# Silu rows at their written place, other PSUM banks and weight slots around attention, and whole quarters in the last opening of a two-layer diffusion backbone

## The chip, the cores and the metric

The kernel runs on one core of one Trainium2 chip, in one launch. The metric is device time of that core in microseconds. The kernel before was run three times: 2442.37, 2443.3 and 2446.17, a median of 2443.3.

## What is computed

Two layers work on 512 latent tokens and a prefix of 256 context tokens, 1024 channels each. Every layer is a half-step SwiGLU, a token mixer (layer 0 a short gated convolution, layer 1 attention with 8 query and 2 key heads of 128) and a second half-step SwiGLU of width 2816. Each of the six sub-layers is an RMSNorm, a shift and scale from a conditioning vector, the sub-layer, and a gated residual. After attention only the latent tokens are left.

```
def norm_modulate(x, g, shift, scale):
    return rms_norm(x, g) * (1 + scale) + shift

def swiglu(h, w_in, w_out):
    gate, up = jnp.split(h @ w_in, 2, axis=-1)
    return (jax.nn.silu(gate) * up) @ w_out
...
        m_lat = (silu_c @ ada_w[i] + ada_b[i]).reshape(b, N_SUBLAYERS, N_MOD, 1, d)
...
        h = norm_modulate(x_lat, norm_g[i, 0], m_lat[:, 0, 0], m_lat[:, 0, 1])
        x_lat = x_lat + MACARON_WEIGHT * m_lat[:, 0, 2] * swiglu(h, ffn_w_in[i, 0], ffn_w_out[i, 0])
...
            y_lat, y_ctx = attention_mixer(h, hc, attn_w_qkv[j], attn_q_g[j], attn_k_g[j], attn_w_o[j],
                                           cos, sin, not last)
...
    return rms_norm(x_lat, final_g)
```

## The kernel before

**Numbers.** Everything is float32. A product is made of three TensorE matmuls (`mm3`, L814 to L816): each operand is split into a high part in TensorE's own 32-bit format, which ScalarE writes by a copy (L186), and a low part, the remainder, which VectorE writes by a subtraction (L187). high × high, low × high and high × low are added up in PSUM. So each weight tile and each activation tile costs ScalarE and VectorE an instruction before TensorE can use it.

**Stages.** They run one after the other under the keys f00 (first SwiGLU, with the start of the kernel, the boot), c01 (convolution), f02, f10, attention, and f12, the last SwiGLU. Large products are taken by Strassen's seven products M1 to M7 over halves of the channels and halves of the tokens; their operands are sums such as T1 to T4 of the four quarters B11, B21, B12 and B22 of the modulated input (first digit: half of the channels, 4 chunks of 128; second digit: half of the tokens). A half of the tokens is 384 up to f10 and 256 in f12. The first few columns of each stage (c0, c1, in the boot c2) are multiplied directly, by quarters, while the sums are still being made.

**Opening.** The norm, the modulation and the splits of a stage are its opening. Per quarter: `normed` (L732, VectorE, x times the root), `modulated` (L745, ScalarE, one instruction for each chunk), `parted` (L769 ScalarE high, L771 VectorE low). Each of these works on pairs of chunks, `PAIRS`: 2 × 384 = 768 elements for each partition, or 2 × 256 = 512 in f12. The sums of quarters (L774) and their splits go by pairs, too. `OPENING` and `behind` in `out_close` list at which step of the products each call stands. The squares (`sq_add`, `ssq`) and the root (`th`, `tl`, `y`, `r`, L589 to L617) come before, for each half of the tokens when its residuals (L882, L952) are done.

**Weights.** SyncE's queue fetches raw weights in 512 KB pieces into 5 `raw` buffers. ScalarE and VectorE split them into 8 buffers `w` (granules of 128 x 512), or into slots of a large buffer (`T0` to `T13`) that other tiles have left. `stream` is their order; an entry with an event isn't split before the event has been traced. `oheld` are six of the output weights of attention's second half of heads, with the event "heads", which is traced at the end of attention. `HELD_AFTER_HEADS` names their slots. `add_out` lists the weights of the down projections, whose first part covers two chunks of the width and whose others cover four (`FFN_PARTS`); an entry for a part of two is 128 x 256.

**Conditioning.** Products of later shifts, scales and gates run on VectorE in the background (L510, `ada_step`), paced behind the products. They need `silu_row`, a row of Silu(c) for each half of its length: GpSimd's queue brings it, ScalarE makes the Silu in place (L495). ScalarE needs its Silu table for it; the root needs the table of Ln and Exp, so it reloads when it turns from one to the other (1283 ns each). The gate of a SwiGLU needs the Silu table as well.

**Order.** TensorE and SyncE's queue run in the written order. VectorE runs in the written order along its chain. ScalarE's instructions are placed by a scheduler, except inside the regions that `in_order` opens (the boot's opening, `out_close` with the opening behind it, the end). So a Silu of a background row can be placed earlier than it is written.

**PSUM.** It has eight banks, given to pools by name: `psum(C=2, O=1)` opens two tiles C of two banks and one bank O, and later pools lie over banks of closed ones in the order in which they are opened. The rotary stage of attention holds Q, two B, four A and S. Attention proper (`scores` L1447, `turn` L1470, `values`) then takes 32 blocks, 4 for each of 8 heads: scores into C, softmax by VectorE and ScalarE into `pr`, six transposes through T into `p`, and every second block the product with the values into O. From the second half of the heads on, T is given up and opened anew beside two banks AB, in which the output projection of the first four heads runs, one output for each block (`filler`). `out_close` then takes the second four heads' part, in two halves of the tokens, with f12's opening behind it.

Of the kernel before, what the change touches and what calls it, by code (L numbers as in the profile page):

```python
# [18 lines left out]
P = 128  # L19
D = 1024  # L20
KC = D // P
# [48 lines left out]
LAST_T_SLOTS = {**T_SLOTS, "T1": (12, 13), "T3": (6, 7)}  # L70
LAST_F_SLOTS = {**F_SLOTS, (0, 0): 6, (1, 0): 7}
HELD_AFTER_LAST_T = ((12, 13), (10, 11), (8, 9))
HELD_AFTER_HEADS = ((4, 5), (8, 9))
# [53 lines left out]
def backbone(ctx: ExitStack, tc: tile.TileContext, a: dict, out: bass.AP):  # L127
# [266 lines left out]
    def w_list():  # L394
# [25 lines left out]
        add_out(a["attn_w_o"], 4, 4, HELD_AFTER_HEADS, "oheld", ("heads", "heads"))  # L420
# [70 lines left out]
    def silu_load(kh):  # L491

        row = silu_row[kh] = apool.tile([P, 2, 512], F32, name=f"silu_row{kh}", tag="acc")
        nc.gpsimd.dma_start(row, a["crow"][kh].unsqueeze(0).to_broadcast((P, 2, 512)))
        act.activation(row, row, AF.Silu)  # L495
# [212 lines left out]
    PAIRS = (slice(0, 2), slice(2, 4))  # L708
# [10 lines left out]
    def opening(i, s):  # L719
# [6 lines left out]
        def normed(half, tok, p):  # L726

# [3 lines left out]
            m = 4 * half + PAIRS[p].start  # L731
            dve.tensor_tensor(out=full[half, tok][:, PAIRS[p]], in0=xs(slice(m, m + 2), off, n), in1=rs[geo.tokens[tok]].unsqueeze(1).to_broadcast((P, 2, n)), op=ALU.mult)  # L732

        def modulated(half, tok, p, mode=None):

            off, n = geo.tokens[tok]
            for k in range(PAIRS[p].start, PAIRS[p].stop):
# [24 lines left out]
        def parted(half, tok, p, which="both", more=0):  # L762
            name = f"B{half + 1}{tok + 1}"
            if p == 0 and which != "lo":
                t_tiles(name, more)
            hi, lo = T[name][0][:, PAIRS[p], : geo.half], T[name][1][:, PAIRS[p], : geo.half]
            src = full[half, tok][:, PAIRS[p]]
# [5 lines left out]
        def minus(o, x, y, p):  # L773
            dve.tensor_tensor(out=o[:, PAIRS[p]], in0=x[:, PAIRS[p]], in1=y[:, PAIRS[p]], op=ALU.subtract)  # L774

        def sums(which, p):
            if which == "T1":
# [12 lines left out]
        def sum_parted(which, p):  # L790
            if p == 0:
                t_tiles(which)
            t_split(which, full[which] if which in full else full[0, 0], PAIRS[p])
# [67 lines left out]

    def out_steps(groups, passes, gh, gl, npart, after, alloc, width):
# [23 lines left out]
        for m0 in range(0, KC, width):  # L886
            ms = range(m0, min(m0 + width, KC))
            units = [w_get() for _ in ms]
# [10 lines left out]
            else:  # L899
# [4 lines left out]
                w_done()  # L904
# [384 lines left out]
    def attention(gp, i, s):  # L1289
# [140 lines left out]
        with tc.tile_pool(name="core", bufs=2) as cp, psum(C=2, O=1), ExitStack() as more:  # L1430
            more.enter_context(psum(T=3))
# [3 lines left out]
            def scores(h, blk):  # L1435
                g = h // 4
                if blk == 0:
# [3 lines left out]
                    st[h] = qh, ql  # L1441
                qh, ql = st[h]
# [19 lines left out]
            def turn(h, blk, pr):  # L1462
# [4 lines left out]
                for c0 in (0, 3):  # L1467
                    pt = ptile("T", (P, 4, P))[:, :3, :]
# [25 lines left out]
            for n, (h, blk) in enumerate(blocks):  # L1494
# [19 lines left out]
            traced.add("heads")  # L1514
# [207 lines left out]
    with tc.tile_pool(name="g2", bufs=1) as gp, tc.tile_pool(name="qp2", bufs=1) as qp, psum(C=3, A=3, B=1, S=1):  # L1722
# [77 lines left out]
```

## Time and profile before

| What | us |
|---|---|
| Median of three runs | 2443.3 |
| The profiled execution | 2442.06 |
| Its span | 2439.9 |
| TensorE's loading of weights busy, beside its matmuls | 2264.6 |
| ScalarE, L186, all splits of weights (868) | 524.9 |
| VectorE, L187, all splits of weights (868) | 577.6 |
| VectorE, L510, conditioning (416) | 313.8 |
| TensorE's longest wait: the first transfer, ada, at the start | 4.3 |

The profiled execution is one run; its span reaches from the first to the last instruction and is 2.16 us shorter than its time. The matmul ends of TensorE are modelled by the profiler, so a busy TensorE may still run slower than it could where its clock is throttled; the granted clock beside a window shows that. In lists of waits a line says which engine, on which line, waited for the result of which other engine and line, with the total, how often, and the longest. Numbers of lines are those of the kernel before.

### The profile page before, as it was taken

Reading aid. Unit: us, or ns where it says so; the run is one execution under the profiler, and the core shown is the slowest. Engines: PE = TensorE matmul, PEld = TensorE weight load, DVE = VectorE, ACT = ScalarE, POOL = GpSimd, SP = SyncE. Lnnn points to the kernel's source line nnn. Section 1 sums busy time; section 2 is a strip of 40 time slices with the busy share of each in tenths; the row PEclk is TensorE's granted clock in tenths of the full one; section 3 lists DMA queues with packets and bytes.
Section 4 is the critical chain, followed back from the end, with each engine's and each line's share of the span. In section 5 each row is a group of like instructions: output and inputs, shape, how many; then the busy total and the mean of one; then the engine's idle time right before and its main releaser. Section 6 shows DMA issues by size and latency. Waiting matters only on the chain.

```text
span 2439.9 us, 37626 instructions
## 1 busy us (share of the span) xinstructions
PE 2396.1 (98%) x14303; PEld 2264.6 (93%) x14303; DVE 2031.1 (83%) x4011; ACT 1166.9 (48%) x2205; POOL 134.6 (6%) x256
## 2 busy tenths in 40 slices
PE   8999999999999999999999999999999999999998
PEld 5899999999999999999999999999997889899997
DVE  5889989978988888888877988788768887887776
ACT  5544344356435643443435534334346776555545
POOL 0001101100000001001000011101100000000000
PEclk9999999999999999999999999999999999999999
DMA  8234433330334023323431134434331101132232
GB/s 312 87 113 125 140 129 122 126 130 26 100 106 133 30 71 115 123 94 114 130 105 60 66 117 132 153 118 136 128 113 61 44 1 48 57 115 102 99 102 78
DMA packets 93061, 253.70 MB, mean 104 GB/s; under 512 B 10320, under 2 KB 18640, under 8 KB 92880
## 3 DMA queue, kind: packets, MB, share of 16 engines
q1 hardware_dynamic: 71984, 183.65, 22.2%
q0 software_dynamic: 20352, 67.12, 8.9%
q8 instruction: 112, 1.84, 0.3%
q14 instruction: 69, 0.57, 0.1%
q10 hardware_dynamic: 544, 0.52, 0.1%
HBM read 249.16 MB, written 2.10 MB: 103 GB/s over the span
## 4 chain that ended last, share of the span: by engine, by line
PE 80%; issue 8%; DVE 6%; ACT 4%; DMA 2%; POOL 0%; SPq 0%; DVEq 0%; ACTq 0%; POOLq 0%
PE ps_A L815 14%; PE ps_A L814 14%; PE ps_A L816 14%; PE ps_C L814 9%; PE ps_C L815 9%; PE ps_C L816 9%; PE ps_B L816 3%; PE ps_B L814 2%; PE ps_B L815 2%; DVE w L187 1%; PE ps_T L1470 1%; DMA raw<-in_ffn_w_in 1%; DMA silu_row<-in_crow 0%; DMA ada<-in_ada_w 0%; ACT f L745 0%
## 5 line engine op out<-in xcount | busy, mean ns | idle before, releaser
L186 ACT ACTIVATE w<-raw 128x512 fp32r<-128x512 f32 (+1 forms) x868 | 524.9, 619 | 735.8 <-PE ps_A L816 294.8
L187 DVE TENSOR_TENSOR w<-raw,w 128x512 fp32r<-128x512 f32 (+1 forms) x868 | 577.6, 679 | 129.6 <-ACT w L186 117.4
L489 POOL DMA_DIRECT2D aw<-in_ada_t x240 | 129.0, 538 | 1389.4 <-DVE mods L510 985.6
L814 PE MATMUL ps_C<-gh,w 128*128 128x512 f32 (+1 forms) x544 | 194.0, 357 | 3.3 <-ACT w L186 2.8
L815 PE MATMUL ps_C<-gl,w 128*128 128x512 f32 (+1 forms) x544 | 193.8, 356 | 0.0
L816 PE MATMUL ps_C<-gh,w 128*128 128x512 f32 (+1 forms) x544 | 193.5, 356 | 0.0
L354 DVE TENSOR_TENSOR raw<-raw,raw 128x512 f32<-128x512 f32 x264 | 181.3, 689 | 11.2 <-DMA raw<-in_ffn_w_in 7.2
L814 PE MATMUL ps_A<-gh,w 128*128 128x256 f32 (+1 forms) x544 | 180.6, 332 | 1.2 <-DVE x L882 1.2
L816 PE MATMUL ps_A<-gh,w 128*128 128x256 f32 (+1 forms) x544 | 180.7, 332 | 0.0
L815 PE MATMUL ps_A<-gl,w 128*128 128x256 f32 (+1 forms) x544 | 180.6, 332 | 0.0
L510 DVE CUSTOM_DVE_ANT_0 ps_S<-aw,silu_row,packed 128x512 f32<-128x512 f32 x208 | 156.9, 754 | 2.2 <-DMA aw<-in_ada_t 0.9
L510 DVE CUSTOM_DVE_ANT_0 ps_S<-aw,silu_row,mods 128x512 f32<-128x512 f32 x208 | 156.9, 754 | 1.0
L882 DVE SCALAR_TENSOR_TENSOR x<-ps_C,gat,x 128x512 f32<-128x512 f32 (+1 forms) x156 | 102.8, 659 | 41.3 <-PE ps_C L816 41.0
L814 PE MATMUL ps_A<-tB11h,w 128*128 128x384 f32 (+1 forms) x400 | 130.7, 327 | 0.2 <-ACT tB11h L754 0.2
L815 PE MATMUL ps_A<-tB11l,w 128*128 128x384 f32 (+1 forms) x400 | 130.4, 326 | 0.2 <-DVE tB11l L755 0.2
L816 PE MATMUL ps_A<-tB11h,w 128*128 128x384 f32 (+1 forms) x400 | 130.4, 326 | 0.0
L815 PE MATMUL ps_C<-tB22l,w 128*128 128x384 f32 (+2 forms) x384 | 124.6, 325 | 0.0
L816 PE MATMUL ps_C<-tB22h,w 128*128 128x384 f32 (+2 forms) x384 | 124.2, 324 | 0.0
L814 PE MATMUL ps_C<-tB22h,w 128*128 128x384 f32 (+2 forms) x384 | 124.0, 323 | 0.0
L814 PEld LDWEIGHTS ps_C<-gh,w 128*128 128x128 f32 x544 | 103.2, 190 | 18.1 <-ACT w L186 4.4
L814 PE MATMUL ps_A<-tT4h,w 128*128 128x384 f32 (+1 forms) x352 | 114.2, 325 | 2.9 <-DVE c L1091 2.9
L882 DVE SCALAR_TENSOR_TENSOR x<-ps_A,gat,x 128x512 f32<-128x512 f32 (+1 forms) x164 | 100.2, 611 | 20.1 <-PE ps_A L816 19.9
(437 smaller groups left out, 6924.2 us busy)
## 6 DMA issues: line engine op xcount, KB each, us to landing
raw<-in_ffn_w_in SPq DMA_DIRECT2D x170, 512.0 KB, 3.7
aw<-in_ada_t POOLq DMA_DIRECT2D x240, 256.0 KB, 2.9
raw<-in_ffn_w_out SPq DMA_DIRECT2D x80, 512.0 KB, 4.1
raw<-in_conv_w_in SPq DMA_DIRECT2D x24, 512.0 KB, 3.5
ada<-in_ada_w SPq DMA_DIRECT2D x28, 256.0 KB, 5.3
raw<-in_attn_w_qkv SPq DMA_DIRECT2D x12, 512.0 KB, 4.8
raw<-in_ada_w SPq DMA_DIRECT2D x8, 512.0 KB, 6.3
silu_row<-in_crow POOLq DMA_DIRECT2D x8, 512.0 KB, 4.2
```

What stands on the lines that cost most here:

```text
L186: act.activation(dsth, src, AF.Copy)
L187: dve.tensor_tensor(out=dstl, in0=src, in1=dsth.bitcast(F32), op=ALU.subtract)
L354: dve.tensor_tensor(out=quad(o), in0=quad(x), in1=quad(y), op=ALU.subtract)
L489: nc.gpsimd.dma_start(w, a["ada_t"][t, kh, j])
L510: ins = dve.tensor_tensor_reduce(out=junk, in0=w, in1=silu_row[kh][:, v, :], scale=1.0, scalar=total if kh else ada_b[:, i, hm // 2, col : ...
L814: pe.matmul(ps, wh, xh, start=first, stop=False, **kw)
L815: pe.matmul(ps, wh, xl, start=False, stop=False, **kw)
L816: pe.matmul(ps, wl, xh, start=False, stop=last, **kw)
L882: dve.scalar_tensor_tensor(out=x, in0=p[:, o - off : o - off + w], scalar=gat[:, m, v : v + 1], in1=x, op0=ALU.mult, op1=ALU.add)
L1470: pe.transpose(pt[:, c, :], pr[:, (c0 + c) * P : (c0 + c + 1) * P], ident)
```

## The change

It makes five edits.

1. The Silu of the conditioning rows keeps its written place in ScalarE's order. It then stands among the products, behind which the conditioning is paced, and in three stages the Silu table is already loaded there, by the gate's first Silu; that load stands in front of the gate in the boot, and in the first eviction of the direct columns in f02 and f10.
2. Attention's pools are opened in another order, O, T (two), C, and with a third transpose bank U for the first four heads; T stays open, U is closed for AB. In the last stage the pools are opened as S, B, A, C.
3. The six kept output weights go to other slots and are split when heads 5 and 7 begin, in the order of the stream, instead of at the end of attention. By the order of the changed kernel, the ScalarE parts stand in blocks 4 to 9 of attention, the VectorE parts in blocks 17 to 25.
4. In f12, whose half is 256 tokens, the opening works on whole quarters: one instruction of 128 x 1024 takes the place of two of 128 x 512, for `normed`, `parted`, the sums and their splits. The second call of each step does nothing there. The slots of f12's operands change with it.
5. Where a part of a down projection covers two chunks, one split of 128 x 512 takes the weights of two outputs, and both outputs read from that granule.

TensorE's instructions and their order stay the same, except that a third of the transposes of the first four heads go to U; so do SyncE's and GpSimd's. ScalarE has 17 instructions fewer, VectorE 21.

```diff
-LAST_T_SLOTS = {**T_SLOTS, "T1": (12, 13), "T3": (6, 7)}
-LAST_F_SLOTS = {**F_SLOTS, (0, 0): 6, (1, 0): 7}
-HELD_AFTER_LAST_T = ((12, 13), (10, 11), (8, 9))
-HELD_AFTER_HEADS = ((4, 5), (8, 9))
+LAST_T_SLOTS = {"B11": (0, 1), "B21": (2, 3), "B12": (6, 7), "T4": (6, 7), "T1": (8, 13), "B22": (9, 10), "T2": (11, 12), "T3": (4, 5)}
+LAST_F_SLOTS = {(0, 0): 4, (1, 0): 5, (0, 1): 11, (1, 1): 12}
+HELD_AFTER_LAST_T = ((8, 13), (11, 12), (9, 10))
+HELD_AFTER_HEADS = ((6, 7), (9, 10))
...
     def add_plain(raw, u, ks, where=None, event=None):
+        both = isinstance(u, slice)
+
         def make(dh, dl):
-            split(dh, dl, raw_tiles[raw][0][:, u, ks])
-            raw_used(raw)
-        stream.append((event, where, ks.stop - ks.start, make))
+            src = raw_tiles[raw][0][:, u, ks]
+            if both:
+                dh, dl = (t.rearrange("p (u k) c -> p u k c", u=2) for t in (dh, dl))
+            split(dh, dl, src)
+            for _ in range(1 + both):
+                raw_used(raw)
+        stream.append((event, where, (ks.stop - ks.start) * (1 + both), make))
...
+            if npart == 2:
+                add_plain(n, slice(0, 2), slice(0, npart))
+                continue
...
-        add_out(a["attn_w_o"], 4, 4, HELD_AFTER_HEADS, "oheld", ("heads", "heads"))
+        add_out(a["attn_w_o"], 4, 4, HELD_AFTER_HEADS, "oheld", ("head5", "head7"))
...
-        act.activation(row, row, AF.Silu)
+        tc.keep_in_program_order(act.activation(row, row, AF.Silu))
...
-    PAIRS = (slice(0, 2), slice(2, 4))
+    def pair(p):
+
+        return slice(2 * p, 2 * p + 2) if geo.half > 256 else slice(0, 4)
...
         def normed(half, tok, p):
-
+            if p and geo.half <= 256:
+                return
...
-            m = 4 * half + PAIRS[p].start
-            dve.tensor_tensor(out=full[half, tok][:, PAIRS[p]], in0=xs(slice(m, m + 2), off, n), in1=rs[geo.tokens[tok]].unsqueeze(1).to_broadcast((P, 2, n)), op=ALU.mult)
+            ks = pair(p)
+            m = 4 * half + ks.start
+            count = ks.stop - ks.start
+            dve.tensor_tensor(out=full[half, tok][:, ks], in0=xs(slice(m, m + count), off, n), in1=rs[geo.tokens[tok]].unsqueeze(1).to_broadcast((P, count, n)), op=ALU.mult)
...
+    def out_unit(m, npart):
+
+        if npart > 2:
+            return w_get()
+        if m % 2 == 0:
+            shared[:] = w_get()
+        return [t[:, npart * (m % 2) : npart * (m % 2) + npart, :] for t in shared]
...
-            units = [w_get() for _ in ms]
+            units = [out_unit(m, npart) for m in ms]
...
-        with tc.tile_pool(name="core", bufs=2) as cp, psum(C=2, O=1), ExitStack() as more:
-            more.enter_context(psum(T=3))
+        with tc.tile_pool(name="core", bufs=2) as cp, psum(O=1, T=2, C=2), ExitStack() as more:
+            more.enter_context(psum(U=1))
+            turns = [0]
...
                     split(qh, ql, qf[h])
                     st[h] = qh, ql
+                    traced.add(f"head{h}")
...
-                    pt = ptile("T", (P, 4, P))[:, :3, :]
+                    turns[0] += 1
+                    pt = ptile("U" if h < 4 and turns[0] % 3 == 0 else "T", (P, 4, P))[:, :3, :]
...
-                        more.enter_context(psum(T=2, AB=1))
+                        more.enter_context(psum(AB=1))
...
-            traced.add("heads")
...
-    with tc.tile_pool(name="g2", bufs=1) as gp, tc.tile_pool(name="qp2", bufs=1) as qp, psum(C=3, A=3, B=1, S=1):
+    with tc.tile_pool(name="g2", bufs=1) as gp, tc.tile_pool(name="qp2", bufs=1) as qp, psum(S=1, B=1, A=3, C=3):
```

`modulated`, `parted`, `minus`, `sums` and `sum_parted` use `pair(p)` and return early for the second pair in the same way as `normed`. A granule that two outputs share is given back behind the second of them.

More of the change, by code (lines that the diff above doesn't have):

```diff
@@ L762, in parted @@
         def parted(half, tok, p, which="both", more=0):
+            if p and geo.half <= 256:
+                return
             name = f"B{half + 1}{tok + 1}"
@@ L765, in parted @@
                 t_tiles(name, more)
-            hi, lo = T[name][0][:, PAIRS[p], : geo.half], T[name][1][:, PAIRS[p], : geo.half]
-            src = full[half, tok][:, PAIRS[p]]
+            hi, lo = T[name][0][:, pair(p), : geo.half], T[name][1][:, pair(p), : geo.half]
+            src = full[half, tok][:, pair(p)]
             if which != "lo":
@@ L773, in minus @@
         def minus(o, x, y, p):
-            dve.tensor_tensor(out=o[:, PAIRS[p]], in0=x[:, PAIRS[p]], in1=y[:, PAIRS[p]], op=ALU.subtract)
+            dve.tensor_tensor(out=o[:, pair(p)], in0=x[:, pair(p)], in1=y[:, pair(p)], op=ALU.subtract)
         def sums(which, p):
+            if p and geo.half <= 256:
+                return
             if which == "T1":
@@ L790, in sum_parted @@
         def sum_parted(which, p):
+            if p and geo.half <= 256:
+                return
             if p == 0:
                 t_tiles(which)
-            t_split(which, full[which] if which in full else full[0, 0], PAIRS[p])
+            t_split(which, full[which] if which in full else full[0, 0], pair(p))
         def squares(tok, ms):
@@ L903, in out_steps @@
                     yield
-                w_done()
+                if npart > 2:
+                    w_done()
+                elif ms[-1] % 2 or m0 + width >= KC:
+                    w_done()
+                else:
+                    last = taken.pop()
+                    w_done()
+                    taken.append(last)
             major = False
```

5 lines of the change are left out of this document (4 added, 1 removed).

## The prediction

> **What bounds the kernel now.** I read the page's busy shares first, then what TensorE waited for, then the chain of waits and the stretches in which TensorE stood idle.
>
> ```profile
> span 2439.9 us, 37626 instructions
> PE 2396.1 (98%) x14303; PEld 2264.6 (93%) x14303; DVE 2031.1 (83%) x4011; ACT 1166.9 (48%) x2205; POOL 134.6 (6%) x256
> ```
>
> TensorE is busy for 2396.1 of 2439.9 us and its work is unchanged, so the change can win at most part of 43.8 us of idle time and of the stretches with a throttled clock. The profiled execution took 2442.06 us (2.16 us outside its span), 1.24 under the median of 2443.3. The sum is made against 2442.06. From the list of TensorE's waits (engine, line, releaser: total, times, longest):
>
> ```profile
> PE ps_A L814 <- ACT tB12h L186: 3.4, 1, 3.4
> PE ps_A L814 <- DVE c L1091: 2.9, 2, 2.0
> PE ps_C L814 <- ACT w L186: 2.8, 1, 2.8
> PE ps_S L616 <- ACT th L609: 2.1, 2, 1.4
> PE ps_C L1447 <- DVE vl L1408: 1.7, 1, 1.7
> PE ps_A L815 <- DVE tB12l L771: 1.7, 5, 0.6
> PE ps_B L816 <- DVE w L187: 1.2, 1, 1.2
> PE ps_A L814 <- DVE o L187: 1.1, 1, 1.1
> ```
>
> Each part of the change aims at some of these.
>
> **Part 1: the Silu rows keep their place.** Unpinned, the scheduler puts the first Silu of a stage and its table load ahead of the opening's modulation (L745). The chain (start, duration, what), and ScalarE's and VectorE's lines in the boot:
>
> ```profile
> 50.98 1.06 ACT silu_row L495
> 52.03 0.99 ACT f L745 x2
> ...
> 566.86 4.25 DMA silu_row<-in_crow
> 571.17 1.28 ACT L495
> ...
> 818.56 3.88 DMA silu_row<-in_crow
> ...
> 1331.20 3.85 DMA silu_row<-in_crow
> ```
> ```profile
> 49.68 1.28 ACT L495 ACT_TABLE_LOAD   x1 [4.25 <-DMA silu_row<-in_crow]
> 47.43 0.95 DVE L732 TENSOR_TENSOR f<-x,r 128x768 f32<-128x768 f32 x1
> ```
>
> ScalarE stood 4.25 us until the row had landed, then loaded a table (1.28) and ran the Silu (1.06), while the normed pair lay ready at 47.43 + 0.95 = 48.4. The modulation began at 51.9 and can now begin 3.5 earlier. In the boot this takes away the 3.4 us wait of TensorE. The clock comes on top:
>
> ```profile
> 50.00:55.00 5.00, 1.36 (x9) 0.28 (x1) 0.98 (x3) 4.92 (x8) 2.12 (x4) 0.83 0.56 199
> 55.00:60.00 5.00, 4.89 (x16) 4.42 (x17) 4.46 (x10) 2.62 (x6) 0.00 (x0) 0.50 0.10 39
> ...
> 2064.00:2068.00 4.00, 4.00 (x23) 4.00 (x23) 3.63 (x8) 1.79 (x5) 0.00 (x0) 0.61 0.00 0
> ...
> 2124.00:2128.00 4.00, 2.01 (x17) 1.83 (x17) 3.38 (x7) 2.08 (x6) 0.00 (x0) 1.00 0.69 210
> ```
>
> The columns are the window, its length, busy time (and count) of TensorE, its weight loads, VectorE, ScalarE and GpSimd, then the granted clock. After the 3.4 us wait the clock was 0.50 for a whole 5 us, so 4.89 busy us did the work of about 2.4. Removing the wait may win up to 2.4 more. Given back: the boot's table load, which moves before the first Silu of the gate (L1169, 1.28 us, just ahead of the 2.8 us wait for w in the same boot), and about 0.4 from the wider output split (part 4). So 3.4 + 1.2 (half of the clock's 2.4, since openings further on still wait) − 1.7 = 2.9; I take 2.5, between 0.5 (nearly all given back) and 5.
>
> In the other three openings the same load and Silu, 2.34 us, stand ahead of the modulation, and TensorE loses what its lead doesn't cover: the recorded waits for tB12l (1.7 over five times), some 1.0 of them here, and at most 1.6 more in the matmuls slowed around them. That loss goes whole; I take 2.2. Two of the stages pay for it with a table load in their eviction, covered except for 0 to 0.5 each. That makes −1.7, between −2.6 and 0.
>
> The Trainium skill (ScalarE: Activation LUTs, What ACT_TABLE_LOAD costs) gives a table switch 1283 ns and some 1380 ns of drain behind it. Here the load starts at 49.68 and the Silu at 50.98, so only the 1.28 shows. With the drain, the boot would give back 1.4 more and the time would come out at about 2437.
>
> **Part 2: attention's banks.**
>
> ```profile
> 1916.21 0.61 ACT L186 ACTIVATE qh<-qf 128x512 fp32r<-128x512 f32 x1
> ...
> 1924.20 0.47 PE L1447 MATMUL ps_C<-kh,qh 128*128 128x512 f32 x1 [1.74 <-DVE vl L1408]
> ```
>
> Before, the score banks lie over those of the last value projections, and the first scores wait 1.74 us for the evictions of these. Afterwards they lie on banks that the rotary stage has long left, and the first head's operand was split eight microseconds earlier. This wait goes: −1.7. The transposes rotate over three buffers as before until the fourth head ends.
>
> **Part 3: the kept output weights.** Six splits move from behind attention into its first third:
>
> ```profile
> 2040.89 3.24 ACT L186 ACTIVATE oheld<-raw 128x512 fp32r<-128x512 f32 x6 [1.55 <-PE ps_A L816]
> ...
> 1926.00:1938.00 12.00, 11.11 (x82) 10.05 (x81) 11.19 (x27) 11.07 (x24) 0.00 (x0) 1.00 0.13 44
> 1938.00:1950.00 12.00, 11.14 (x81) 9.99 (x80) 10.62 (x27) 9.78 (x21) 0.00 (x0) 1.00 0.13 46
> 1986.00:1998.00 12.00, 12.00 (x85) 11.07 (x84) 8.57 (x19) 7.84 (x16) 0.00 (x0) 1.00 0.00 1
> ```
>
> After attention they no longer stand in front of the last head's eviction and of the eight ordinary splits: about half of the 1.1 us wait for o goes (0.55), the 1.4 us wait for th goes, because the weights behind it are there, and with it the stretch at clock 0.61, which cost 4 × 0.39 = 1.56. Together −3.5 ahead of the last opening. In attention VectorE does its halves where it has a third free (8.57 of 12), but ScalarE's six (3.24) fall, by their order, into blocks 4 to 9 of 32, 1938 to 1955, where 2.2 of 12 us are free and TensorE already idles 0.86. Cost between 0 and 1.5; I take 0.7. Parts 2 and 3 within attention: −1.0.
>
> A rule speaks on the clock: the Trainium skill (TensorE: Matmul & The Clock Gate, Part 1) says that only about a whole idle window of 3.4 us halves it. The 3.4 us wait in the boot agrees, the 2.0 idle us of 2124 to 2128 at clock 1.00 too; the 0.61 after an idle 1.4 us does not. By the rule alone the 1.56 would stay and the time would be 2437.5.
>
> **Part 4: the last opening by whole quarters.** The durations, by shape (mean ns), and where the second half's chain begins and ends:
>
> ```profile
> L187 DVE TENSOR_TENSOR tT1l<-f,tT1h 128x768 fp32r<-128x768 f32 x2 | 1.8, 956 | 0.2 <-ACT tT1h L186 0.2
> L187 DVE TENSOR_TENSOR w<-raw,w 128x256 fp32r<-128x256 f32 x2 | 0.8, 418 | 0.0
> L187 DVE TENSOR_TENSOR w<-raw,w 128x512 fp32r<-128x512 f32 x1 | 0.7, 685 | 0.0
> ...
> L186 ACT ACTIVATE tT1h<-f 128x768 fp32r<-128x768 f32 x2 | 1.6, 838 | 0.0
> L186 ACT ACTIVATE w<-raw 128x256 fp32r<-128x256 f32 x4 | 1.3, 400 | 0.0
> L186 ACT ACTIVATE w<-raw 128x512 fp32r<-128x512 f32 x1 | 0.6, 624 | 0.0
> ```
> ```profile
> 2082.66 1.29 DVE L732 TENSOR_TENSOR f<-x,r 128x512 f32<-128x512 f32 x2
> 2085.06 1.08 ACT L745 ACTIVATE f<-f,mods,scl 128x256 f32<-128x256 f32 x2
> 2090.13 0.69 DVE L771 TENSOR_TENSOR tB22l<-f,tB22h 128x512 fp32r<-128x512 f32 x1 [0.96 <-ACT tB22h L769]
> ```
>
> Continuing from 512 to 768 by another 256 elements, 1024 cost 1.22 on VectorE and 1.05 on ScalarE; four modulations cost 2 × 1.08. A quarter is then a serial chain of 1.22 + 2.16 + 1.05 + 1.22 = 5.6 us, and the next quarter's norm stands behind its last step on VectorE. Two quarters take 11.3, less about 0.8 of overlaps of consecutive instructions: 10.5. Before, the pairs interleaved and the two took 2090.82 − 2082.66 = 8.2. So the second half ends 2.3 later by itself. In the first half VectorE's turns were shared with the evictions, and the serial form fits into what it took. With part 3's 3.5 in hand and about 0.7 lost to evictions that now stand behind a whole quarter, the last tB22l comes some 0.5 us earlier than before. TensorE and VectorE behind it:
>
> ```profile
> 2092.00:2096.00 4.00, 4.00 (x36) 4.00 (x35) 3.75 (x8) 2.69 (x7) 0.00 (x0) 1.00 0.00 0
> ...
> 2092.00:2124.00 32.00, 30.01 (x202) 27.30 (x201) 31.56 (x60) 17.09 (x40) 0.00 (x0) 1.00 0.17 58
> ```
>
> At 36 matmuls in 4 us the 24 that a quarter feeds take 2.7 us. Against chains of 5.6 TensorE sees waits of up to 2.6 us, where it had at most 0.6, and reaches the first product later by about 1.5. But from 2092 to 2124 VectorE is busy for 31.56 of 32 us, and TensorE idles for it 2.0 there and 2.0 more up to 2128 (2.9 for c, 1.2 for w). So VectorE sets the end of that stretch. It saves 8 × 0.07 (two 512-wide calls cost 1.29, one of 1024 1.22) and, by the wider splits of the first output part, 4 × (2 × 0.42 − 0.69) = 0.6. In the other stages these wider splits save the same behind a busy TensorE: nothing. Parts 3 and 4 after attention: −0.5 − 0.6 − half of 0.6 = −1.4, taken as −1.5; between −3.5 (the refill behind 2124 is earlier too) and +3 (TensorE, late at the products, doesn't catch up, and 1.5 for the clock).
>
> **Sum:** −2.5 − 1.7 − 1.0 − 1.5 = −6.7, so 2435.4 on the profiled execution's own time and 2436.6 on the median. I forecast 2436.
>
> **The rivals.**
> *All of it lands:* the boot wins its full clock (−5), the openings −2.6, attention −1.7 and the last −3.5: −12.8, or about 2430. For it: the 0.50 window. Against: the table load in front of w.
> *Given back:* the boot's gain goes into the stretch where w was late by 2.8 anyway (−0.5), the clock at 2064 stays (+1.5), the rest as forecast: −3.7 + 1.5, or 2440, within the noise.
> *Serial quarters decide:* TensorE is late at the products and stalls there still. +3 instead of −1.5, and boot and openings at half, −2.1: with −1.0, no change, 2442. For it: four waits of 2.6. Against: a VectorE without a gap behind them.
> *The wait moves instead of going (slower):* the row's transfer (4.25, 3.88, 3.85 us) isn't issued earlier, and the pinned Silu may stand on it at its new place, with the hi parts of the weights queued behind it and TensorE behind these. ScalarE then stands some 4 us in each of four stages, 16 in all; it decides as soon as the eight split weights ahead don't cover them. Without cover 2435.4 + 16 = 2451. Against it, from the view of the Silu's line:
>
> ```profile
>   DMA silu_row<-in_crow: 15.7, 8
> ```
>
> Of eight Silus the four hoisted ones account for these 15.7 us (3.9 each); the other four ran at such places already and waited for nothing.
>
> **How the numbers follow.** Forecast 0.50, all lands 0.14, given back 0.16, serial quarters 0.14, moved wait 0.06. About 0.2%, 4.9 us, is what a measurement tells from no change; so faster means under 2438.4 against the median. Faster: 0.47 of the forecast's 0.50 and the 0.14, 0.61. Same: the 0.03, the 0.16 and 0.12 of the serial quarters, 0.31. Slower: 0.06 and 0.02 of the serial quarters, 0.08. The range 2429 to 2444 leaves out the moved wait, the upper end of the serial quarters and a little below, under 2 in 10.
>
> **What would show it.** Right: no 3.4 us wait in the boot and a clock near 1.00 at 55 to 60; no silu_row transfer in the chain; no wait at L1447 for vl; four VectorE calls of 128x1024 near 1.22 and waits of 2 to 3 us for tB21l, tB12l and tB22l; a gapless VectorE behind these that ends earlier counted from the end of attention. Wrong: ScalarE waiting for silu_row inside the products; TensorE idle over 1 us more in attention's first third; a halved clock in the last opening; the last stage, from attention's end, longer than before.

## The result, and the profile after

| | median us | runs | range |
|---|---|---|---|
| before | 2443.66 | 7 | 2442.37 to 2446.17 |
| changed | 2450.58 | 7 | 2448.37 to 2453.43 |

The ratio is 1.0027, with a 95% interval of 1.0016 to 1.0038: the change makes the kernel slower by 6.9 us (0.3%), where 7 us less were forecast, and the time lies 6.6 us above the range. The profiled execution took 2450.91 us, with a span of 2449.1.

In the changed kernel some lines have other numbers: L835 to L837 are the three matmuls L814 to L816, L913 is the residual's eviction L882, L746 the norm L732, L760 the modulation L745, L786 and L788 the high and low part L769 and L771, L598 and L599 the squares L589 and L590, L504 the Silu row. In the kernels of the experiments they shift by a few again: L901 is the eviction, L743 the norm, L783 and L785 the high and low part, L832 to L834 the matmuls. From the page, and the larger of TensorE's waits behind the first transfer:

```profile
span 2449.1 us, 37563 instructions
PE 2396.9 (98%) x14303; PEld 2266.1 (93%) x14303; DVE 2029.6 (83%) x3979; ACT 1163.6 (48%) x2181; POOL 134.6 (5%) x256
```
```profile
PE ps_A L835 <- DVE x L913: 11.2, 5, 4.3
PE ps_S L483 <- ACT adr L479: 2.8, 3, 1.4
PE ps_C L835 <- ACT w L186: 2.8, 1, 2.8
PE ps_A L836 <- DVE tB11l L788: 1.9, 1, 1.9
PE ps_A L836 <- DVE tB21l L788: 1.8, 1, 1.8
PE ps_A L835 <- ACT tB12h L786: 1.8, 1, 1.8
PE ps_A L835 <- DVE c L1129: 1.7, 2, 1.0
```

TensorE does the same work in the same busy time, and stands idle for 52 us instead of 44. The waits that the change aimed at are gone: 3.4 for tB12h in the boot, 1.7 for vl, 1.4 for th, 1.1 for o. On top of the list is 11.2 us for the eviction of x, five times. In the kernel before this line was:

```profile
PE ps_A L814 <- DVE x L882: 1.9, 2, 1.2
```

Three waits of 1.8 to 1.9 us stand in the last opening. And a wait for adr, a row of the conditioning that ScalarE copies for TensorE, has grown from 0.7 us to 2.8, all of it in the boot.

By the two pages ScalarE has 24 instructions fewer (2205 and 2181) and VectorE 32 (4011 and 3979), not the 17 and 21 named with the change.

**Where the time went.** TensorE's matmuls come in the same order in both kernels, so the same matmul can be found in both traces and its two starts subtracted. That gives the lead (−) or lag (+) at each place. The last two columns are from two experiments below.

| At (us in the trace of before) | changed | without the shared split | that, with pairs |
|---|---|---|---|
| 45, ahead of the first Silu's old place | +1.4 | −0.1 | −0.1 |
| 106, end of the boot's opening | −3.5 | −3.8 | −3.1 |
| 118, behind f00's first output part | +3.7 | −3.7 | −2.2 |
| 832, behind f02's opening | +1.8 | −5.6 | −4.0 |
| 870, behind f02's first output part | +5.3 | −5.3 | −3.7 |
| 1345, behind f10's opening | +4.6 | −6.0 | −4.4 |
| 1385, behind f10's first output part | +8.1 | −5.7 | −4.0 |
| 1926, first scores of attention | +6.3 | −7.5 | −5.8 |
| 2040, end of attention | +7.7 | −5.9 | −4.3 |
| 2068, the close, ahead of the quarters | +2.6 | −11.0 | −9.4 |
| 2092, behind the last quarter | +12.6 | −1.1 | −8.7 |
| 2150, last stage under way | +10.0 | −2.5 | −8.5 |
| 2424, near the end | +9.6 | −3.2 | −9.1 |

Rows of a traced execution carry about 1 us of chance from the first transfers (the first row). Steps within a column don't carry that, but a stretch of 3.4 us at half the clock, worth some 1.7 us, can fall into one execution and not into another of the same code. Two things cost: the first output part of f00, f02 and f10 (+7.1, +3.5, +3.5), and the quarters of the last opening (+10.0). Of the rest, the boot's opening gains 4.9 us, the next three 2.6 and the close 5.1; attention gains 1.8 at its first scores and loses 1.5 in its first third.

**The first output part.** VectorE's timeline in f02 (start, busy time, line, operation, tiles, count), first of the changed kernel, then the same place of the kernel before:

```profile
856.67 0.75 DVE L913 SCALAR_TENSOR_TENSOR x<-ps_C,gat,x 128x512 f32<-128x512 f32 x1
857.33 1.89 DVE L187 TENSOR_TENSOR w<-raw,w 128x512 fp32r<-128x512 f32 x3
859.13 0.75 DVE L913 SCALAR_TENSOR_TENSOR x<-ps_A,gat,x 128x512 f32<-128x512 f32 x1
859.79 0.75 DVE L913 SCALAR_TENSOR_TENSOR x<-ps_C,gat,x 128x512 f32<-128x512 f32 x1
```
```profile
852.23 0.42 DVE L187 TENSOR_TENSOR w<-raw,w 128x256 fp32r<-128x256 f32 x1
852.57 0.75 DVE L882 SCALAR_TENSOR_TENSOR x<-ps_C,gat,x 128x512 f32<-128x512 f32 x1
853.23 0.74 DVE L882 SCALAR_TENSOR_TENSOR x<-ps_A,gat,x 128x512 f32<-128x512 f32 x1
853.89 0.74 DVE L882 SCALAR_TENSOR_TENSOR x<-ps_C,gat,x 128x512 f32<-128x512 f32 x1
```

Before, the three evictions of x follow each other from 852.57 on. Now three splits of weights, 1.89 us, stand between the first and the second, and TensorE, out of PSUM banks, restarts at 859.93 when the second has ended. By the order of the instructions these aren't the output's weights: one is M6's of the column that runs, two are those of the next column's M1 and M2. A part of eight outputs used to take eight granules, as many as there are. With two outputs in one it takes four, and the routine that fills free granules writes splits of later weights into VectorE's order that much sooner, ahead of evictions on which TensorE waits. VectorE has no gap there, so each split in front is a split's delay (window, length, busy time of TensorE, its loads and VectorE):

```profile
855.00:860.00 5.00, 2.09 (x16) 1.81 (x14) 5.00 (x9) 2.71 (x5) 0.00 (x0) 1.00 0.51 193
```

In the boot the wait for x is 4.3 us, and the clock falls behind it (the first two lines are the boot's opening):

```profile
50.00:55.00 5.00, 3.63 (x21) 1.97 (x20) 4.26 (x9) 4.17 (x8) 2.12 (x4) 1.00 0.77 270
55.00:60.00 5.00, 5.00 (x34) 3.66 (x38) 3.09 (x7) 3.36 (x8) 0.00 (x0) 1.00 0.52 148
110.00:115.00 5.00, 2.60 (x9) 2.41 (x10) 5.00 (x10) 1.43 (x2) 0.00 (x0) 0.63 0.00 0
115.00:120.00 5.00, 5.00 (x22) 4.14 (x22) 4.32 (x8) 1.26 (x2) 0.00 (x0) 0.69 0.00 0
```

At 55 to 60 the clock is 1.00, as forecast for the pinned Silu (it was 0.50). At 110 to 120 it is 0.63 and 0.69, where it was 1.00 in both windows before. TensorE was busy for 5.7 us at half the clock there (111.3 to 118.1), which makes, as an estimate, 2.9 of the 7.1 us that this output part loses.

**The quarters.** VectorE's and ScalarE's timelines of the changed kernel, first half of the last opening and then the second, and the first and last VectorE line of the first half in the kernel before:

```profile
2069.50 1.22 DVE L746 TENSOR_TENSOR f<-x,r 128x1024 f32<-128x1024 f32 x1
2074.27 0.42 DVE L599 TENSOR_TENSOR ssq<-ssq,sq 128x256 f32<-128x256 f32 x1 [3.15 <-ACT sq L598]
2075.01 1.22 DVE L788 TENSOR_TENSOR tB11l<-f,tB11h 128x1024 fp32r<-128x1024 f32 x1
2076.14 1.22 DVE L746 TENSOR_TENSOR f<-x,r 128x1024 f32<-128x1024 f32 x1
...
2081.63 1.22 DVE L788 TENSOR_TENSOR tB21l<-f,tB21h 128x1024 fp32r<-128x1024 f32 x1
...
2090.72 1.23 DVE L746 TENSOR_TENSOR f<-x,r 128x1024 f32<-128x1024 f32 x1
2095.18 1.23 DVE L788 TENSOR_TENSOR tB12l<-f,tB12h 128x1024 fp32r<-128x1024 f32 x1 [3.23 <-ACT tB12h L786]
...
2100.77 1.23 DVE L788 TENSOR_TENSOR tB22l<-f,tB22h 128x1024 fp32r<-128x1024 f32 x1 [3.23 <-ACT tB22h L786]
```
```profile
2070.76 2.08 ACT L760 ACTIVATE f<-f,mods,scl 128x256 f32<-128x256 f32 x4 [2.67 <-DVE f L746]
2072.87 1.06 ACT L786 ACTIVATE tB11h<-f 128x1024 fp32r<-128x1024 f32 x1
2073.84 0.40 ACT L598 ACTIVATE sq<-x 128x256 f32<-128x256 f32 x1
```
```profile
2066.05 0.69 DVE L732 TENSOR_TENSOR f<-x,r 128x512 f32<-128x512 f32 x1
...
2075.73 0.68 DVE L771 TENSOR_TENSOR tB21l<-f,tB21h 128x512 fp32r<-128x512 f32 x1
```

A call of 1024 takes 1.22 to 1.23, as estimated, and a quarter is the serial chain that was priced: norm at 2069.50, low part done at 2076.2. Two things weren't priced. On VectorE the sum of a square (ssq, 2074.27) stands ahead of the next eviction, and ScalarE makes that square (2073.84) only behind the whole quarter, so VectorE is idle for 3.15 us there instead of evicting. And each half is longer: 13.4 us in the first (2069.50 to 2082.85) where it was 10.4 (2066.05 to 2076.41), 11.3 in the second (2090.72 to 2102.0) where it was 8.2, with 1.6 more between them.

### The profile page after: what moved, and what is told of

Read it like the earlier page. It is cut to its first block, busy times and chain, and to the rows that moved or that the text cites. A ratio compares the mean times of both kernels' runs of the same rounds, so it can differ in the third digit from the quotient of the medians.

```text
span 2449.1 us, 37563 instructions
## 1 busy us (share of the span) xinstructions
PE 2396.9 (98%) x14303; PEld 2266.1 (93%) x14303; DVE 2029.6 (83%) x3979; ACT 1163.6 (48%) x2181; POOL 134.6 (5%) x256
## 4 chain that ended last, share of the span: by engine, by line
PE 85%; DVE 7%; ACT 4%; DMA 3%; issue 1%; SPq 0%; DVEq 0%; ACTq 0%
PE ps_A L835 15%; PE ps_A L836 15%; PE ps_A L837 15%; PE ps_C L835 10%; PE ps_C L836 10%; PE ps_C L837 10%; PE ps_B L835 2%; PE ps_B L837 2%; PE ps_B L836 2%; DVE w L187 1%; DMA ada<-in_ada_w 1%; DMA raw<-in_ffn_w_in 1%; ACT f L760 1%; DMA raw<-in_ffn_w_out 1%; DVE f L746 1%
## 5 line engine op out<-in xcount | busy, mean ns | idle before, releaser
L186 ACT ACTIVATE w<-raw 128x512 fp32r<-128x512 f32 x852 | 525.0, 627 | 750.7 <-PE ps_A L837 291.5
L187 DVE TENSOR_TENSOR w<-raw,w 128x512 fp32r<-128x512 f32 x852 | 577.7, 689 | 138.1 <-ACT w L186 125.1
L835 PE MATMUL ps_C<-gh,w 128*128 128x512 f32 (+1 forms) x544 | 194.7, 358 | 4.0 <-ACT w L186 2.8
L837 PE MATMUL ps_C<-gh,w 128*128 128x512 f32 (+1 forms) x544 | 193.7, 356 | 0.0
L835 PE MATMUL ps_A<-gh,w 128*128 128x256 f32 (+1 forms) x544 | 182.1, 335 | 10.6 <-DVE x L913 10.5
L837 PE MATMUL ps_A<-gh,w 128*128 128x256 f32 (+1 forms) x544 | 181.4, 334 | 0.0
L913 DVE SCALAR_TENSOR_TENSOR x<-ps_C,gat,x 128x512 f32<-128x512 f32 (+1 forms) x156 | 102.9, 660 | 42.0 <-PE ps_C L837 41.7
L835 PE MATMUL ps_A<-tB11h,w 128*128 128x384 f32 (+1 forms) x400 | 131.2, 328 | 0.2 <-ACT tB11h L769 0.2
L837 PE MATMUL ps_A<-tB11h,w 128*128 128x384 f32 (+1 forms) x400 | 130.7, 327 | 0.0
L835 PEld LDWEIGHTS ps_A<-gh,w 128*128 128x128 f32 x544 | 104.0, 191 | 23.0 <-DVE x L913 11.8
L837 PE MATMUL ps_C<-tB22h,w 128*128 128x384 f32 (+2 forms) x384 | 124.3, 324 | 0.0
L835 PE MATMUL ps_C<-tB22h,w 128*128 128x384 f32 (+2 forms) x384 | 124.1, 323 | 0.0
L835 PEld LDWEIGHTS ps_C<-gh,w 128*128 128x128 f32 x544 | 103.5, 190 | 18.7 <-ACT w L186 5.1
L837 PEld LDWEIGHTS ps_C<-gh,w 128*128 128x128 f32 x544 | 103.4, 190 | 15.1 <-DVE w L187 0.2
```

Source lines behind the costliest of these rows:

```text
L186: act.activation(dsth, src, AF.Copy)
L187: dve.tensor_tensor(out=dstl, in0=src, in1=dsth.bitcast(F32), op=ALU.subtract)
L835: pe.matmul(ps, wh, xh, start=first, stop=False, **kw)
L837: pe.matmul(ps, wl, xh, start=False, stop=last, **kw)
L913: dve.scalar_tensor_tensor(out=x, in0=p[:, o - off : o - off + w], scalar=gat[:, m, v : v + 1], in1=x, op0=ALU.mult, op1=ALU.add)
```

## The experiments

Each ratio is taken against the kernel before on the same chip. The first four rows come from one chip (before 2444.2), the next six from a second (2443.8, for the last two of them 2443.4), the last two from a third (2443.8). So a difference between rows of different chips carries up to 0.9 us more of uncertainty.

| Kernel | median us | ratio to before, 95% interval |
|---|---|---|
| pinned Silu rows alone | 2440.06 | 0.9984, 0.9975 to 0.9993 |
| shared split alone | 2452.42 | 1.0034, 1.0021 to 1.0047 |
| changed, no shared split | 2440.22 | 0.9983, 0.9974 to 0.9992 |
| changed, shared split counted as two | 2438.88 | 0.9981, 0.9971 to 0.9990 |
| no shared split, pairs | 2432.19 | 0.9952, 0.9938 to 0.9965 |
| counted as two, pairs | 2429.76 | 0.9945, 0.9932 to 0.9957 |
| no shared split, quarters overlapped | 2432.61 | 0.9957, 0.9945 to 0.9970 |
| no shared split, pairs, kept splits pinned | 2431.46 | 0.9950, 0.9937 to 0.9962 |
| pinned Silu rows and banks | 2438.18 | 0.9977, 0.9968 to 0.9986 |
| counted, pairs, kept splits pinned | 2430.18 | 0.9946, 0.9934 to 0.9959 |
| no shared split, quarters overlapped, made once | 2433.48 | 0.9958, 0.9945 to 0.9970 |
| counted, quarters overlapped, made once | 2432.72 | 0.9952, 0.9939 to 0.9966 |

**The pinned Silu alone**, on the kernel before.

```diff
-        act.activation(row, row, AF.Silu)
+        tc.keep_in_program_order(act.activation(row, row, AF.Silu))
```

> The kernel before with the pinned Silu rows alone. Main theory (the shared output granule lets later weights be split ahead of the residual's evictions, and that alone turns the change into a loss): the pin is pure gain, some 4 us in the boot by the alignment of the two traces and 2.2 in the three other openings: 2437.5, 6 us under the kernel before. Rival (the pinned Silu waits for its row inside the products, or the moved table load eats the boot's gain): 2443 to 2447, no gain.

It gains 4.2 us. Matched matmul by matmul, it leads by 4.9 us at 61, gives back some 2 up to 98 and keeps 3.8 at 106; the other openings add 2.6. One us is lost at attention's first scores, where the clock was halved for 3.4 us in this execution, and 2 in the last stage. So the direction holds, and the size is two thirds of the expected.

**The shared split alone**, on the kernel before: `add_out`, `add_plain`, `out_unit` and the giving back of granules as in the change.

> The kernel before with the shared granule of the two-chunk output parts alone. Main theory: waits of TensorE for the eviction of x of 2.9 to 4.3 us in the first output part of f00, f02 and f10 and a halved clock behind the first, together 12 to 14 us: 2456. Rival (the stalls in these output parts come with the pinned Silu rows, which moved the ScalarE order of these stages): within 1 us of the kernel before.

It loses 8.2 us, less than expected, and shows the wait without any of the other edits:

```profile
PE ps_A L823 <- DVE x L901: 9.8, 5, 3.9
```

**The change without it.**

```diff
-            if npart == 2:
-                add_plain(n, slice(0, 2), slice(0, npart))
-                continue
...
-            units = [out_unit(m, npart) for m in ms]
+            units = [w_get() for _ in ms]
```

> The changed kernel with the splits of the two-chunk output parts as before (one for each output), all else kept. Main theory: the three waits for x go and with them 12 to 14 us: 2437, some 6 us under the kernel before. Rival (silu rows): 2449 to 2451, as the changed kernel.

10.4 us less than the changed kernel (10.9 when each is taken against the kernel before beside it). The waits for x at the three output parts are gone, as the table of leads shows; the rest of the change is worth only 4, because the quarters take most of what is left.

**The shared split kept, but counted as two granules.** The work is that of the changed kernel; only when later weights may be split differs.

```diff
-                add_plain(n, slice(0, 2), slice(0, npart))
+                add_plain(n, slice(0, 2), slice(0, npart), "two")
...
-            if where is None and state["open"] >= GRANULES:
+            if where in (None, "two") and state["open"] + (1 if where is None else 2) > GRANULES:
...
-            if where is None:
-                state["open"] += 1
+            if where in (None, "two"):
+                state["open"] += 1 if where is None else 2
```

> The changed kernel with the shared granule kept, but counted as two of the eight in the look-ahead, so that no later weights are split earlier than before. Main theory (order on VectorE): the waits for x go although the splits are 128x512 and shared, 2437 to 2439. Rival (the wider split itself is late for the first output, or a granule held for two outputs blocks the next): waits of 2 us and more stay in the first output parts, 2447 to 2451.

2438.88: 11.7 us less than the changed kernel, with the same wide splits and shared granules. VectorE's timeline in f02:

```profile
846.91 0.67 DVE L187 TENSOR_TENSOR w<-raw,w 128x512 fp32r<-128x512 f32 x1
847.51 0.74 DVE L913 SCALAR_TENSOR_TENSOR x<-ps_C,gat,x 128x512 f32<-128x512 f32 x1
848.17 0.73 DVE L913 SCALAR_TENSOR_TENSOR x<-ps_A,gat,x 128x512 f32<-128x512 f32 x1
848.83 0.73 DVE L913 SCALAR_TENSOR_TENSOR x<-ps_C,gat,x 128x512 f32<-128x512 f32 x1
```

The evictions follow each other again. So neither the width of the split nor the held granule costs, but the order that the free granules bring about. Of all runs this one decides the cause.

**Pairs instead of quarters**, without the shared split. `pair(p)` returns two chunks always and the early returns go.

```diff
-        return slice(2 * p, 2 * p + 2) if geo.half > 256 else slice(0, 4)
+        return slice(2 * p, 2 * p + 2)
```

> The changed kernel without the shared split and with the last opening by pairs of chunks again; pinned Silu, banks, kept weights and slots stay. Theory (quarters are a serial chain that puts TensorE's first products some 10 us later against the end of attention's output, of which VectorE's later work swallows only a part): the 9 us that the trace without the shared split has in hand at the start of the last opening stay for most of it, 2434 to 2436, 4 to 6 under that kernel's 2440.2. Rival (VectorE sets the end of that stretch whatever the opening does): within 1 us of 2440.

2432.19, 8.0 less than the same kernel with quarters (7.6 when each is taken against the kernel before on its own chip). In the table it leads by 9.4 at 2068, by 8.7 at 2092 and by 9.1 near the end: what the close gains stays to the end. So the rival that VectorE sets the end of the stretch whatever the opening does, which was the forecast's own reasoning, fails.

**The same with the shared split counted as two.**

> As the run before, with the shared split counted as two granules instead of none. Theory: the shared split, rid of its look-ahead, saves a little VectorE and ScalarE time, 0 to 1.5 us under the run before, 2433 to 2436. Rival: no difference, or slower, because the first output waits for a split of twice the width.

2429.76, 2.4 less than without the shared split, a little more than expected. The intervals overlap widely, so that the shared split helps is likely, not shown.

**Quarters with the steps overlapped**: the second quarter's norm stands ahead of the first one's low part, its modulation right behind the first one's high part.

```diff
+            late = ("normed", 1, 0, 0)
+            behind[4].remove(late)
+            behind[3].insert(0, late)
...
+            table[2, 1] = [("normed", 0, 1, 0), ("normed", 1, 1, 0), ("modulated", 0, 1, 0, "short"), ("parted", 0, 1, 0, "hi")]
+            table[2, 2] = [("parted", 0, 1, 0, "lo"), ("modulated", 1, 1, 0, "short"), ("parted", 1, 1, 0, "hi")]
+            table[2, 3] = [("parted", 1, 1, 0, "lo")]
```

> The changed kernel without the shared split, whole quarters kept, but the second quarter's norm ahead of the first quarter's low part in both halves, so that ScalarE modulates one quarter while VectorE subtracts in the other. Theory (the serial order, not the width, costs): a half takes 8.6 instead of 10.5 us, 2437 to 2438.5, half of what pairs win. Rival (the width costs: a quarter has to be whole before TensorE can start on it): 2439.5 to 2441, no gain.

2432.61: 7.6 less than the serial quarters (7.2 against the kernel before on each chip), more than expected. Its second half on VectorE:

```profile
2075.76 2.36 DVE L743 TENSOR_TENSOR f<-x,r 128x1024 f32<-128x1024 f32 x2
...
2080.22 1.23 DVE L785 TENSOR_TENSOR tB12l<-f,tB12h 128x1024 fp32r<-128x1024 f32 x1 [2.10 <-ACT tB12h L783]
...
2083.28 2.48 DVE L785 TENSOR_TENSOR tB22l<-f,tB22h 128x1024 fp32r<-128x1024 f32 x2 [1.83 <-ACT tB22h L783]
```

The two norms run back to back, and the half ends at 2084.5, 8.8 us behind its start, where the serial form took 11.3. The last row counts two: the edit left the call for the last low part at its old place as well, so VectorE made it twice.

**The same, made once.** The line for step (2, 3) goes, and the call at (3, 0) stays as it is in the changed kernel.

> The run with overlapped quarters made the last quarter's low part twice on VectorE (1.23 us), an instruction that the edit left at its old place. Here it is made once, all else the same (no shared split). Theory (the serial order costs, the width doesn't): 0.5 to 1.2 us under that run's 2432.6, 2431.5 to 2432, level with pairs (2432.2) or a little under them. Rival (the opening isn't on the path there, VectorE's repeated part was hidden): 2432.6.

2433.48, on another chip: not less, as the rival says, so the repeated part was most likely hidden. Its lag against the kernel before grows by 3.6 us from 2068 to 2092 and is back to 2.5 at 2150, against 9.9 and 8.6 with serial quarters and 0.8 and 1.0 with pairs. The overlap takes back most of the loss, and a remainder stays. TensorE's waits in the last opening of this kernel show it:

```profile
PE ps_A L833 <- DVE tB11l L785: 1.9, 1, 1.9
PE ps_A L832 <- ACT tB12h L783: 1.8, 1, 1.8
```

Each half's first quarter still has to be whole before TensorE can take its first chunk.

**The kept splits pinned to their place**, with pairs and without the shared split.

```diff
-    def split(dsth, dstl, src):
-        act.activation(dsth, src, AF.Copy)
+    def split(dsth, dstl, src, pinned=False):
+        hi = act.activation(dsth, src, AF.Copy)
+        if pinned:
+            tc.keep_in_program_order(hi)
...
-            split(dh, dl, src)
+            split(dh, dl, src, where is not None and where[0] == "oheld")
```

> The first of these runs with ScalarE's six kept splits pinned to their written place in attention's second half. Theory (hoisted into attention's first third they cost 1.5 us there, where ScalarE and VectorE have no room): 1 to 2 us under the first of these runs. Rival (that loss comes from the transposes' third bank or from chance): no difference.

2431.46 against 2432.19, with ranges that overlap: not told apart by the times. In the traces the loss between 1926 and 1978 is 0.8 us instead of 1.5.

**Pinned Silu and the banks**, without the kept weights' new place.

> The kernel before with the pinned Silu rows and attention's banks in their new order, with the third transpose bank U, but the kept weights behind attention as before. Theory (the rest of the loss in attention's first third belongs to the kept weights and the two ordinary splits that come with them): the wait for vl goes, 1.7 us, and all of it is still there at the end of attention; 2438.3, 1.7 under the pin alone. Rival (the banks or U cost 0.7 us themselves): 2439.

2438.18, 1.9 under the pin alone, but only 1.0 when each is taken against the kernel before on its own chip, and the two intervals overlap. In the trace the lead grows by 1.8 at the first scores, and then loses 0.8 up to 1978 with no kept splits there. So the rival is right for that half: some 0.8 of the 1.5 in attention's first third comes with the banks or with running ahead into blocks where ScalarE and VectorE have no room, and the other 0.7 with the hoisted splits. Which of the first two it is stays open.

**All that helped.**

> All that helped: pinned Silu rows, new banks, kept weights with ScalarE's parts pinned to their written place, pairs of chunks in the last opening, and the shared split counted as two granules. Theory (the parts add up): 0.7 under the counted version's 2429.8, 2429. Rival (the pinned ScalarE parts come late for the end of attention in this version): 2430 to 2432.

2430.18, the same as without the pinned kept splits (2429.76). They add nothing that can be measured. These two versions are the fastest here, 13 to 14 us under the kernel before and 20 to 21 under the changed one.

**The change with two repairs**: the shared split counted as two, the quarters overlapped and made once.

> The changed kernel with the two repairs: the shared split counted as two granules, and the quarters' steps overlapped, each made once. Theory (the five edits are sound and only what they let happen to the order costs): 2429 to 2430, level with pairs and the counted split (2429.8). Rival (quarters cost by their width): 2431 to 2433.

2432.72, 17.9 less than the changed kernel, but 3.0 more than the same with pairs (2429.76 on another chip with the same median of before; ranges apart: 2431.50 to 2434.39 against 2429.36 to 2431.04). This goes to the rival: whole quarters cost here even when their steps overlap, some 1 to 3 us, where an instruction less on VectorE for each pair wins nothing that shows.

## Why the prediction was wrong, point by point

**The shared split, priced at nothing outside the last stage: this is the step that failed.** The prediction said that in the other stages the wider splits "save the same behind a busy TensorE: nothing", apart from 0.4 given back in the boot. It counted instructions and their durations and left out what the granules that they free would trigger. The trace counts 14.1 us of lag in the three output parts (7.1 + 3.5 + 3.5), 8.2 for the edit alone and 10.4 to 11.7 for taking it or its look-ahead out of the changed kernel. VectorE takes its instructions in the written order, and in that order splits of later weights stand ahead of evictions; no term of the sum covers that.

**The last opening, forecast at −1.5 with the close in front of it, was about +2.2** (from +7.7 at 2040 to +10.0 at 2150). The close itself was right in mechanism and too small in size: −5.1 in the trace against −3.5. The term that failed is the lag of the quarters, priced at 3.0 (2.3 and 0.7) and measured at 10.0 from 2068 to 2092. "In the first half … the serial form fits into what it took" is the wrong sentence: that half took 13.4, not 10.4, and VectorE stood 3.1 us twice there for squares that queue behind a quarter on ScalarE. The second half took the full 11.3 of its chain; the 0.8 of overlaps that the prediction took off did not come. And "VectorE sets the end of that stretch" was misread: VectorE is busy all through it, but its work starts when the opening ends, so a late opening shifts it whole. Only 2.6 of 10.0 came back by 2150. With pairs 1.0 is lost there in all. The rival "serial quarters decide" had this mechanism, at +3 for the stretch instead of +2.2, and was given 0.14.

**The boot**, −2.5: −4.9 in the trace up to the first output part, −3.8 with the pin alone. The wait of 3.4 went, and the wait for w behind the moved table load is 2.8 us as before. But the clock's term of 1.2 is not what the traces show. At 61 the lead has grown by 4.9 us in the changed kernel, where the clock stayed at 1.00, and by 3.3 in the traces with pairs (no shared split) and with pin and banks, where it was halved for 3.4 us at 54. At 83 all of them have gained 3.5, because a TensorE that is early waits 1.4 us for adr (at 64.7 in the changed kernel). So the clock won nothing that lasts here. What comes behind 83 differs from trace to trace with the places of the halved stretches.

**The three other openings**, −1.7: −2.6 in the traces.

**Attention**, −1.0: −1.8 at the first scores, +1.5 in the first third (0.7 forecast, bound 1.5), −0.3 in all.

**The moved wait**, forecast as the slower rival with 0.06, did not come. The argument against it misread its line, though: of the 15.7 us the four hoisted rows had 8.7 (4.3, 1.7, 1.4, 1.3), and the other four waited 7.1 (0.8, 2.0, 2.4, 1.9) at such places already. From the view of the Silu's line in the changed kernel, and from ScalarE's timeline there, a row that moved and one that did not:

```profile
  DMA silu_row<-in_crow: 4.9, 3
```
```profile
892.91 1.05 ACT L504 ACTIVATE silu_row<-silu_row 128x1024 f32<-128x1024 f32 x1
690.41 1.06 ACT L504 ACTIVATE silu_row<-silu_row 128x1024 f32<-128x1024 f32 x1 [2.05 <-DMA silu_row<-in_crow]
```

The four moved rows (at 142, 635, 893 and 1408) wait for nothing. The 4.9 us belong to three rows that waited at the same places before, and TensorE has no wait behind them. The change was slower for another reason, one that none of the rivals named.

**A slip in a rival's sum.** "Given back" leaves out attention's −1.0: its terms give −4.7 + 1.5 = −3.2, not −3.7 + 1.5. On the median that is 2440.1, so its 2440 stands.

## What to carry to other kernels

An edit that frees buffers sooner also starts whatever fills them sooner: where the fill runs on an engine that works in written order, look at what it now stands in front of, and bound the look-ahead by what it was rather than by what fits. Merging two instructions into one of twice the width saves a little fixed cost on each engine, but where the instructions alternate between two engines it takes away the overlap, and the first consumer waits for the whole; starting the next unit's first step ahead of the last step of the one before wins most of that back, not all. An engine that is busy without a gap behind a serial chain doesn't hide the chain if its own work can only start at the chain's end.

## What the runs showed of the hardware

```profile
2073.95:2077.36 3.41, 1.50 (x13) 1.31 (x12) 3.09 (x5) 0.29 (x1) 0.00 (x0) 1.00 0.00 0
2077.36:2080.77 3.41, 3.41 (x18) 3.20 (x16) 0.39 (x1) 3.35 (x7) 0.00 (x0) 0.50 0.02 5
2080.77:2084.18 3.41, 1.57 (x11) 1.37 (x12) 3.27 (x8) 2.58 (x7) 0.00 (x0) 1.00 0.00 0
2084.18:2087.60 3.42, 3.42 (x18) 3.42 (x17) 2.28 (x5) 0.51 (x1) 0.00 (x0) 0.50 0.37 109
2094.43:2097.84 3.41, 1.77 (x12) 1.57 (x13) 2.36 (x2) 0.98 (x2) 0.00 (x0) 1.00 0.00 0
2097.84:2101.25 3.41, 3.28 (x15) 2.82 (x13) 0.48 (x1) 3.36 (x6) 0.00 (x0) 0.50 0.00 0
```

The granted clock (behind GpSimd's column) has only the values 1.00 and 0.50 in these traces, and apart from the start and the end of the kernel it is 0.50 in stretches of 3.41 us or twice that; a value like 0.63 above is a mean over a window. In the last opening of the changed kernel three such stretches follow 3.41 us in which TensorE was busy for 1.50, 1.57 and 1.77 us, behind waits of at most 1.9 us each. The Trainium skill (TensorE: Matmul & The Clock Gate, Part 1) expects that only after an idle window of about 3.4 us; by these rows 1.6 to 1.9 idle us within 3.41 are enough. A sharp bound doesn't come out of the traces: in the kernel before, 1.6 idle us were followed by half the clock (2063.74 to 2067.15) and 1.8 were not (2128.59 to 2132.00). In the changed kernel TensorE fell 1.5, 0.9 and 1.2 us further behind in the three stretches while its matmuls ran. Behind the first and the third it waited for the next quarter (tB21l, tB22l), where a faster TensorE would have waited longer. Behind the second stands the sum for the next half's root (L625, L626): it began at 2087.97, 0.9 us after its operand tl was ready (2087.03). So the clock made, as an estimate, at most 0.9 of the quarters' lag of 10.0; the forecast had it as a bound, with 1.5.
